# Layer norm between two attentions with tokens on partitions; softmax weights scaled by GpSimd before their transpositions

## The chip, the cores and the metric

The kernel runs on one core of a Trainium2 chip. The metric is device time in microseconds (us) of one execution, as the median of several runs.

## The reference

One layer of a first block (gated convolution, dilated attention, feed-forward) is followed by two layers of a second block, over 512 tokens of width 1024 in fp32. Three attentions over 16 heads of 64 follow each other. The first two are softmax attentions, the third is a stick-breaking one. What the change touches:

```python
# softmax attention (layers 1 and 2): per head and query, over the keys
p = exp(scores - max); o = (p @ v) / sum(p)
# layer 2: select keys, attend, gate, project, then the layer norm
p = softmax(logits); o = p @ v
x = layer_norm(ALPHA * x + (o * silu(g)) @ w_out, ln_g, ln_b)
# layer 3: stick-breaking attention on that x, its own gate, projection and layer norm

def layer_norm(x, g, b):
    mu = mean(x, axis=-1); var = mean((x - mu) ** 2, axis=-1)
    return (x - mu) * rsqrt(var + LN_EPS) * g + b
```

## The kernel before, in words

**Layout.** Activations lie with channels on partitions: eight tiles of 128 channels x 512 tokens. Every tensor that goes into a projection is kept as a pair h, l of rounded parts, and every weight block (8 x 128 rows of 128 columns) as a pair hi, lo. A chunk of a projection (`Product.chunk`, lines 302 to 304) is three matmuls, hi*h, hi*l and lo*h, and a projection of one channel tile has eight chunks.

**Weights.** The queue SP loads a block into one of two buffers `wraw`; ScalarE (ACT) rounds it to `whi` (line 120) and GpSimd (POOL) subtracts for `wlo` (line 124), in the second half of the kernel in four pieces of 256 columns. Splits run two blocks ahead of use; there are four buffers of each part.

**Order.** TensorE's (PE) order is that of the program, written out by hand. `pe` is a stream of chunks; `pe.pull(n)` issues the next n, and `pe.after(n, fn)` calls fn once n more chunks have been issued. The other engines' queues are ordered by a planner from program order and expected readiness, and each engine then works strictly in its queue's order.

**Softmax loops** (`pair_loop`, from about 184 to 390 us and 1028 to 1217 us). Eight pairs of heads, each head one slot. In a slot, the scores of its four query tiles alternate with the transpositions (`turn`) and the value products (`weigh`) of the head before, with projection chunks of coming heads pulled in between. `SoftmaxPair.weights` takes the scores to `P` with their maximum on VectorE (DVE, line 627), then ACT the exponential with its sum `den` (line 629, shown as line 193). `turn` transposes the weights of a group of key tiles on PE (line 594), group (0,) first, and ACT and DVE split the result (596, 597). `weigh` multiplies by the values (513). `joined` (519, 520) puts the two halves into `f`. The sums are handled apart: once per pair, `widen` takes the reciprocals and spreads them over 64 columns each (633, 635), `denominators` transposes them on PE (640) and copies them with a factor 0.5 (642), and `finish1` or `finish2` multiplies `f` by them (944; 1480 and 1481 with the gate).

**The layer norm between layers 2 and 3** (`Between`, from about 1217 to 1290 us). `Outward` holds the output projection in this order: four opened channel tiles, two whole ones, and the last two in two halves of 256 tokens each. Every finished tile is added to the residual (line 1212, POOL made the residual's sum in 1207), which calls `summed`. With channels on partitions a token's mean is a sum over partitions, which PE does with a matrix of ones: a provisional mean from four tiles (`middle`, 1242 and 1243), then per half the sums and squares of the shifted tiles (`shift`, 1252 to 1263; `stats`, 1286 and 1287). Each half of each tile is normalised (1299, 1300) and split (1301, 1302) for the next projection. Behind it PE computes three gate products of layer 3 in halves (`gates` with `halved`, 1140): 24 chunks per half.

**The last layer norm** (`Last`) already turns its tiles: PE transposes them (1315), ACT copies (1316), DVE takes statistics along the free axis (1322, 1344).

Of the kernel before, what the change touches and what calls it, by code (L numbers as in the profile page):

```python
# [18 lines left out]
S = 512  # L19
# [32 lines left out]
STATS = (9, 14)  # L52
# [97 lines left out]
def model_kernel(ctx: ExitStack, tc: tile.TileContext, x, norm1_g, w_in, gate_b, conv_w, conv_b, conv_norm_g,  # L150
# [21 lines left out]
    def ps_t():  # L172
        return ps("pt", 3)
# [46 lines left out]
    ones_h = const.tile([128, 128], F32R, name="ones_h")  # L220
# [203 lines left out]
    with tc.tile_pool(name="rows", bufs=1) as rows, tc.manual_schedule(engines={  # L424
# [19 lines left out]
        nc.vector.tensor_scalar(ones_h, zero128, 2.0 / D, None, op0=OP.add)  # L444
# [119 lines left out]
    class HeadPair:  # L564
# [3 lines left out]
        def __init__(self, tmps, pool, qk, v):  # L568
            self.tmps, self.pool, self.qk, self.v = tmps, pool, qk, v
            self.P, self.parts, self.o = {}, {}, {}  # L570
# [28 lines left out]
        def weigh(self, r, group):  # L599
# [17 lines left out]

    class SoftmaxPair(HeadPair):
# [11 lines left out]

        def widen(self):
            rinv = self.pool.tile([128, 2, NT], F32, name="rinv", bufs=2)
            nc.vector.reciprocal(rinv, self.den)
            self.wide = tmp(self.tmps).rearrange("p (t r d) -> p t r d", t=NT, r=2)
            nc.vector.tensor_copy(self.wide, rinv.rearrange("p r t -> p t r")[:, :, :, None].to_broadcast([128, NT, 2, 64]))

        def denominators(self):
            pb = ps_t()
            for qt in range(NT):
                nc.tensor.transpose(pb[:, 128 * qt:128 * qt + 128], self.wide[:, qt].rearrange("p a b -> p (a b)"), ident)  # L640
            self.rb = tmp(self.tmps)
            nc.scalar.activation(self.rb, pb, AF.Copy, scale=0.5)

        def ended(self):
            self.finish(self.f, self.rb)
# [21 lines left out]
    def pair_loop(pair, stream_of, pulls, last=lambda: None):  # L667


        def slot(head, turns, weighs, widen, pulls):  # L670
# [17 lines left out]
            if widen:  # L688
                widen()

        turns = weighs = [None] * 3
        for c in range(ND):
            stream_of(c)
            pr = pair(c)
            for r in range(2):
                slot((pr, r), turns, weighs, pr.widen if r else None, pulls[2 * c + r - 2 * ND] if c >= ND - 2 else pulls[0] if c or r else FIRST)
# [6 lines left out]
        slot(None, turns, weighs, None, DRAIN[1:])  # L703
# [83 lines left out]
    with tc.tile_pool(name="mix1", bufs=1) as mix1:  # L787
# [119 lines left out]
        with tc.tile_pool(name="loop1", bufs=1) as lp:  # L907
# [34 lines left out]
            def finish1(c):  # L942
                def finish(f, rb):
                    nc.vector.tensor_mul(o32[:, c, :], f, rb)
                return finish

            def pair1(c):
# [12 lines left out]
                return SoftmaxPair(lp, lp, (qk[0], qk[1]), lambda: qk["v"], lambda r, qt: B[r][:, 384 - 128 * qt:], finish1(c))  # L960
# [193 lines left out]
    def gated(pool, into, f, c, already, scale=1.0):  # L1154

        def parts():
            if not already:
                nc.vector.tensor_mul(f, f, gs[c])
# [5 lines left out]
        if already or c in gs:  # L1164
# [56 lines left out]
    class Between(Outward):  # L1221

        def summed(self, c, ts):
            part = self.part
            if c == 1:
                nc.vector.tensor_add(part, self.es[0], self.es[1])
            elif c in (2, 3):
                nc.vector.tensor_add(part, part, self.es[c])  # L1230
            if c == 3:
                h, l = act_pair(self.pool, "st", 2)
                nc.scalar.copy(h, part)
                nc.vector.tensor_sub(l, part, f32(h))
                pe.after(4, lambda: self.middle(h, l))
            self.ready.append((c, ts))
            if self.centred:
                self.shift(c, ts)

        def middle(self, h, l):  # L1240
            pm = ps_t()
            nc.tensor.matmul(pm, ones_h, h, start=True, stop=False)
            nc.tensor.matmul(pm, ones_h, l, start=False, stop=True)
            nc.scalar.copy(self.mid, pm)
            self.centred = True
            for a in self.ready:
                self.shift(*a)

        def shift(self, c, ts):
            t = slice(*ts)  # L1250
            es, s1, s2 = [e[:, t] for e in self.es], self.s1[:, t], self.s2[:, t]
            nc.vector.tensor_sub(es[c], es[c], self.mid[:, t])
            eng = nc.gpsimd if c < 4 else nc.vector
            if c == 0:
                nc.scalar.activation(s2, es[c], AF.Square)
            else:
                sq = self.pool.tile([128, S], F32, name="sq", bufs=3)[:, t]
                nc.scalar.activation(sq, es[c], AF.Square)
                if c == 5:
                    eng.tensor_add(s1, es[4], es[5])  # L1260
                elif c > 5:
                    eng.tensor_add(s1, s1, es[c])
                eng.tensor_add(s2, s2, sq)
            if c == ND - 1:
                half = TS.index(ts)
                pe.after(STATS[half], lambda: self.stats(half))

        def normed(self, pool, ys, prods):

            self.pool, self.ready, self.centred, self.ys = pool, [], False, ys  # L1270
            self.mid, self.part, self.s1, self.s2, self.var = (pool.tile([128, S], F32, name=n)
                                                               for n in ("mid", "part", "s1", "s2", "var"))
            self.run()
            for half in range(2):
                pe.together(*[p[half] for p in prods])
            pe.finish()

        def stats(self, half):
            t = slice(*TS[half])
            n = S // 2  # L1280
            p1, p2 = ps_t()[:, :n], ps_t()[:, :n]
            for p, s in ((p1, self.s1), (p2, self.s2)):
                h, l = (a[:, :n] for a in act_pair(self.pool, "st", 2))
                nc.scalar.copy(h, s[:, t])
                nc.vector.tensor_sub(l, s[:, t], f32(h))
                nc.tensor.matmul(p, ones_d, h, start=True, stop=False)
                nc.tensor.matmul(p, ones_d, l, start=False, stop=True)
            mu, var = self.part[:, t], self.var[:, t]
            nc.scalar.activation(var, p1, AF.Square)
            nc.vector.tensor_copy(mu, p1)  # L1290
            nc.vector.tensor_sub(var, p2, var)
            act(var, var, AF.Ln, bias=eps5)
            act(var, var, AF.Exp, scale=-0.5)
            for c, e in enumerate(self.es):
# [294 lines left out]
```

## Time and profile before

| | before |
|---|---|
| median of 3 runs | 1583.32 us (1580.19 to 1585.54) |
| the profiled execution | 1582.75 us |
| its span, first to last instruction | 1580.9 us |
| TensorE busy | 96% of the span |
| mean granted TensorE clock | 0.986 |

Busy time is the time in which an engine has an instruction; matmuls overlap in the pipeline, so their single durations add up to more than the time that they take. In a row, `[1.28 <-ACT Ah]` is idle time of that engine before the instruction and what ended it; `x4` stands for four instructions merged in one row.

### The profile page before, as it was taken

What the parts mean: (1) busy time and instruction counts of PE and PEld (TensorE: products, weight loads), DVE (VectorE), ACT (ScalarE), POOL (GpSimd) and SP (SyncE); (2) the same over time, 40 slices, a digit from 0 to 9 for tenths busy, and PEclk for the clock granted to TensorE, in tenths of its full rate; (3) what the DMA queues carried; (4) which work ended last, traced back from release to release, by engine and by line L of the source; (5) the groups of instructions that cost most, each with busy time, mean ns of one, the idle gap of its engine ahead of it and who ended that gap; (6) DMA issues with size and microseconds to landing.
All of it is one profiled execution on the core that took longest, in us unless ns stands there. A gap on an engine that the chain in (4) does not pass through costs nothing.

```text
span 1580.9 us, 21344 instructions
## 1 busy us (share of the span) xinstructions
PE 1519.2 (96%) x7870; PEld 1290.7 (82%) x7870; DVE 1133.5 (72%) x1867; ACT 827.1 (52%) x1495; POOL 767.0 (49%) x650
## 2 busy tenths in 40 slices
PE   7999999998999999999999989999999789999996
PEld 5888888887878888888888878888887678888885
DVE  8996578777867567627726679988887765777764
ACT  4454678777343443424424344376665445666642
POOL 3687533333735644454454464544552875334324
PEclk9999999999999999999999999999999799999998
DMA  4333321211324333243332342322220313212212
GB/s 142 91 107 93 107 68 41 80 54 54 98 75 119 108 93 89 85 120 94 93 107 87 95 121 68 93 57 78 62 59 14 95 53 94 68 54 81 67 54 80
DMA packets 234604, 130.37 MB, mean 82 GB/s; under 512 B 5206, under 2 KB 232774, under 8 KB 234500
## 3 DMA queue, kind: packets, MB, share of 16 engines
q1 hardware_dynamic: 234356, 128.75, 27.9%
q8 instruction: 62, 1.02, 0.3%
q14 instruction: 42, 0.34, 0.1%
q10 hardware_dynamic: 144, 0.26, 0.0%
HBM read 126.90 MB, written 2.10 MB: 82 GB/s over the span
## 4 chain that ended last, share of the span: by engine, by line
PE 57%; DVE 25%; ACT 8%; issue 4%; POOL 3%; DMA 3%; SPq 0%; DVEq 0%; ACTq 0%; POOLq 0%
PE pj L302 9%; PE pj L303 9%; PE pj L304 9%; DVE pt L832 6%; PE s L303 5%; PE s L302 5%; PE s L304 5%; PE o L513 3%; POOL wlo L124 2%; PE pt L594 2%; PE pj L326 2%; PE pj L328 2%; PE pj L327 2%; PE s L583 1%; DVE score L1445 1%
## 5 line engine op out<-in xcount | busy, mean ns | idle before, releaser
L124 POOL TENSOR_TENSOR wlo<-wraw,whi 128x256 fp32r<-128x256 f32 (+2 forms) x548 | 654.2, 1218 | 698.7 <-ACT whi L120 655.0
L120 ACT CAST whi<-wraw 128x1024 fp32r<-128x1024 f32 (+3 forms) x255 | 243.9, 965 | 243.9 <-PE pj L303 79.0
L302 PE MATMUL pj<-Ah,whi 128*128 128x512 f32 (+3 forms) x896 | 359.5, 401 | 3.7 <-DVE v L719 2.1
L304 PE MATMUL pj<-Ah,wlo 128*128 128x512 f32 (+3 forms) x896 | 348.3, 389 | 2.8 <-POOL wlo L124 2.8
L303 PE MATMUL pj<-Al,whi 128*128 128x512 f32 (+3 forms) x896 | 348.5, 389 | 0.0
L304 PEld LDWEIGHTS pj<-Ah,wlo 128*128 128x128 f32 (+1 forms) x896 | 168.9, 189 | 39.2 <-POOL wlo L124 4.1
L302 PEld LDWEIGHTS pj<-Ah,whi 128*128 128x128 f32 (+1 forms) x896 | 169.5, 189 | 29.1 <-DVE Al L475 1.8
L303 PEld LDWEIGHTS pj<-Al,whi 128*128 128x128 f32 (+1 forms) x896 | 169.6, 189 | 23.9
L832 DVE SCALAR_TENSOR_TENSOR pt<-S,cw,pt 128x494 f32<-128x494 f32 (+26 forms) x210 | 141.8, 733 | 5.5 <-ACT pt L825 3.5
L302 PE MATMUL s<-Ah,whi 128*128 128x512 f32 (+1 forms) x352 | 136.6, 388 | 7.8 <-ACT Ah L1301 4.0
L303 PE MATMUL s<-Al,whi 128*128 128x512 f32 (+1 forms) x352 | 136.3, 387 | 3.7 <-DVE Al L1302 3.7
L304 PE MATMUL s<-Ah,wlo 128*128 128x512 f32 (+1 forms) x352 | 135.9, 386 | 0.0
L326 PE MATMUL pj<-whi,Ah 128*128 128x256 f32 x384 | 112.4, 293 | 1.3 <-DVE q L534 1.3
L597 DVE TENSOR_TENSOR PTl<-pt,PTh 128x512 fp32r<-128x512 f32 x144 | 85.9, 597 | 32.7 <-ACT PTh L596 31.7
L328 PE MATMUL pj<-whi,Al 128*128 128x256 f32 x384 | 108.5, 282 | 0.0
L327 PE MATMUL pj<-wlo,Ah 128*128 128x256 f32 x384 | 108.3, 282 | 0.0
L193 ACT ACTIVATE P<-P,nm 128x128 f32<-128x128 f32 (+3 forms) x128 | 72.0, 563 | 62.9 <-DVE nm L627 61.7
L745 DVE SCALAR_TENSOR_TENSOR u<-ur,fw,u 128x511 f32<-128x511 f32 x44 | 74.9, 1705 | 37.5 <-ACT u L744 37.5
L302 PEld LDWEIGHTS s<-Ah,whi 128*128 128x128 f32 x352 | 68.0, 193 | 21.9 <-ACT Ah L1301 4.6
L596 ACT CAST PTh<-pt 128x512 fp32r<-128x512 f32 x144 | 73.1, 513 | 19.1 <-PE pt L594 18.7
L303 PEld LDWEIGHTS s<-Al,whi 128*128 128x128 f32 x352 | 68.1, 194 | 17.1 <-DVE Al L1302 4.6
L594 PE MATMUL pt<-ident,P 128*128 128x128 f32 x480 | 76.7, 273 | 2.5 <-ACT P L193 0.9
(334 smaller groups left out, 3181.2 us busy)
## 6 DMA issues: line engine op xcount, KB each, us to landing
wraw<-in_w_in_dram SPq DMA_DIRECT2D x56, 512.0 KB
wraw<-in_w_up_dram SPq DMA_DIRECT2D x44, 512.0 KB
wraw<-in_w_in_a_dram SPq DMA_DIRECT2D x36, 512.0 KB
wraw<-in_w_in_b_dram SPq DMA_DIRECT2D x32, 512.0 KB
wraw<-in_w_down_dram SPq DMA_DIRECT2D x16, 512.0 KB
wraw<-in_w_attn_out_dram SPq DMA_DIRECT2D x8, 512.0 KB
wraw<-in_w_conv_out_dram SPq DMA_DIRECT2D x8, 512.0 KB
wraw<-in_w_out_dram SPq DMA_DIRECT2D x8, 512.0 KB
```

Source lines behind the costliest of these rows:

```text
L120: nc.scalar.copy(h, s)
L124: nc.gpsimd.tensor_sub(l[:, k], s[:, k], h[:, k].bitcast(F32))
L302: nc.tensor.matmul(o, hv[:, k, :], ah, start=first, stop=False)
L303: nc.tensor.matmul(o, hv[:, k, :], al, start=False, stop=False)
L304: nc.tensor.matmul(o, lv[:, k, :], ah, start=False, stop=last)
L326: nc.tensor.matmul(o, ah, hv, start=k == 0, stop=False)
L327: nc.tensor.matmul(o, ah, lv, start=False, stop=False)
L328: nc.tensor.matmul(o, al, hv, start=False, stop=k == 7)
L594: nc.tensor.transpose(pt[:, at:at + 128], self.P[r][:, k0:k0 + 128], ident)
L597: nc.vector.tensor_sub(l[:, :at], pt[:, :at], f32(h)[:, :at])
L745: nc.vector.scalar_tensor_tensor(u[:, 1:], v[:, :S - 1], fw[:, 1, j:j + 1], u[:, 1:], op0=OP.mult, op1=OP.add)
L832: nc.vector.scalar_tensor_tensor(o, a, w, o, op0=OP.mult, op1=OP.add)
```

## The change

Two parts. First, in both softmax loops the weights `P` are divided by their sums before they are transposed: a reciprocal of 128x1 on VectorE and a product with two scalars on GpSimd, per head and query tile; `widen`, `denominators` and the products with the reciprocals go. Second, `Between` now works as `Last` does: a common class `Turned` transposes the tiles, takes the statistics along the free axis, and `Between.finish` normalises them with tokens on partitions; `back` transposes each channel tile back and applies gain and bias. `back(c)` is called 7 + 2c chunks after `finish`.

```diff
-STATS = (9, 14)
+BACK = (7, 2)
...
     class HeadPair:
...
         def weigh(self, r, group):
...
-                if r == 0:
+                if r == 0 and self.f is None:
                     self.f = tmp(self.tmps)
...
-        def widen(self):
-            pass
-
-        def denominators(self):
-            pass
...
     class SoftmaxPair(HeadPair):
...
             act(pp, pp, AF.Exp, bias=m, scale=-1.0, accum_out=d)
-
-        def widen(self):
...
-        def denominators(self):
...
+            nc.vector.reciprocal(d, d)
+            nc.gpsimd.tensor_scalar(pp, pp, d, 0.5, op0=OP.mult, op1=OP.mult)

         def ended(self):
-            self.finish(self.f, self.rb)
+            self.finish(self.f)
...
     def pair_loop(pair, stream_of, pulls, last=lambda: None):
...
-            if widen:
-                widen()
...
-                if r:
-                    weighs[1] = lambda pr=pr: (pr.weigh(1, GROUPS[1]), pr.denominators())
...
-            def finish1(c):
-                def finish(f, rb):
-                    nc.vector.tensor_mul(o32[:, c, :], f, rb)
-                return finish
...
+                pr.f = o32[:, c, :]
...
-    def gated(pool, into, f, c, already, scale=1.0):
+    def gated(pool, into, f, c, scale=1.0):

         def parts():
-            if not already:
-                nc.vector.tensor_mul(f, f, gs[c])
+            nc.vector.tensor_mul(f, f, gs[c])
...
-    class Between(Outward):
...
-    class Last(Outward):
+    class Turned(Outward):
...
+        def scales(self, ts):
+            rstd = self.rstd[:, ts[0]:ts[-1] + 1]
+            for t in ts:
+                nc.vector.bn_aggr(self.mv[:, t], self.stats[:, t])
+            act(rstd, self.mv[:, ts[0]:ts[-1] + 1, 1], AF.Ln, bias=eps5)
+            act(rstd, rstd, AF.Exp, scale=-0.5)
+
+    class Between(Turned):
...
+        def finish(self, ts):
+            self.scales(ts)
+            mv, rstd, off = self.mv, self.rstd, self.off
+            for t in ts:
+                nc.vector.scalar_tensor_tensor(off[:, t:t + 1], mv[:, t, 0:1], -1.0, rstd[:, t:t + 1], op0=OP.mult, op1=OP.mult)
+            for k in range(0, D, 512):
+                for t in ts:
+                    z = self.y[:, t, k:k + 512]
+                    if t % 2:
+                        nc.scalar.activation(z, z, AF.Identity, bias=off[:, t:t + 1], scale=rstd[:, t:t + 1])
+                    else:
+                        nc.vector.tensor_scalar(z, z, mv[:, t, 0:1], rstd[:, t:t + 1], op0=OP.subtract, op1=OP.mult)
+            for c in range(ND):
+                pe.after(BACK[0] + BACK[1] * c, lambda c=c: self.back(c, ts))
+
+        def back(self, c, ts):
+            if ts[0] == 0:
+                self.ys.append(act_pair(keep, "A", ND))
+            pt = ps_t()[:, :S // 2]
+            for i, t in enumerate(ts):
+                nc.tensor.transpose(pt[:, 128 * i:128 * i + 128], self.y[:, t, 128 * c:128 * c + 128], ident)
+            h, l = (a[:, 128 * ts[0]:128 * ts[-1] + 128] for a in self.ys[c])
+            g, b = lng[:, c:c + 1], lnb[:, c:c + 1]
+            e = self.pool.tile([128, S // 2], F32, name="e", bufs=3)
+            nc.scalar.activation(h, pt, AF.Identity, bias=b, scale=g)
+            if c % 2:
+                nc.scalar.activation(e, pt, AF.Identity, bias=b, scale=g)
+            else:
+                nc.vector.tensor_scalar(e, pt, g, b, op0=OP.mult, op1=OP.add)
+            nc.vector.tensor_sub(l, e, f32(h))
...
-            def finish2(c):
...
             def pair2(c):
...
-                                   lambda r, qt: maskb[:, OFF[qt]:OFF[qt] + 128 * (qt + 1)], finish2(c), 0.125)
+                                   lambda r, qt: maskb[:, OFF[qt]:OFF[qt] + 128 * (qt + 1)],
+                                   lambda f: gated(dp, og, f, c), 0.125)
```

## Rows read from the trace of the kernel before

**Rows 1.** The page's first part: busy us, share of the span, instructions.

```profile
PE 1519.2 (96%) x7870; PEld 1290.7 (82%) x7870; DVE 1133.5 (72%) x1867; ACT 827.1 (52%) x1495; POOL 767.0 (49%) x650
```

**Rows 2.** Windows: loop 1's body, loop 2's tail, the layer norm; columns as headed.

```profile
core 0: us, PE busy (x) PEld busy (x) DVE busy (x) ACT busy (x) POOL busy (x), PEclk, DMA share, GB/s
184.00:340.00 156.00, 154.95 (x935) 136.02 (x934) 118.98 (x247) 123.20 (x263) 60.09 (x74) 1.00 0.22 65
...
1185.00:1217.00 32.00, 30.20 (x166) 24.38 (x165) 23.20 (x54) 20.44 (x50) 4.31 (x4) 1.00 0.06 17
...
1217.00:1290.00 73.00, 58.27 (x328) 51.73 (x327) 57.08 (x82) 29.28 (x50) 55.50 (x57) 0.86 0.20 58
```

**Rows 3.** Waits of PE, 1217 to 1290 us: total us, times, longest.

```profile
PE pt L1286 <- ACT sth L1284: 5.1, 2, 4.7
PE s L302 <- ACT Ah L1301: 4.0, 3, 2.2
PE s L303 <- DVE Al L1302: 3.7, 4, 1.6
...
```

**Rows 4.** Chain of waits (start, us) at line 640; the group of the copy of line 642.

```profile
1213.20 0.46 PE pt L640 x4
...
L642 ACT ACTIVATE tmp<-pt 128x512 f32<-128x512 f32 x16 | 9.3, 584 | 4.3 <-PE pt L640 4.3
```

**Rows 5.** Timeline of an ordinary slot of loop 2: start us, us, instruction.

```profile
1108.85 0.19 ACT L193 ACTIVATION_READ_ACCUMULATOR P<-P,nm 128x1 f32 x1
...
1111.67 0.60 PE L594 MATMUL pt<-ident,P 128*128 128x128 f32 x4
```

**Rows 6.** Groups of POOL operations by form: busy us, mean ns.

```profile
L1207 POOL TENSOR_TENSOR S<-Ah,Al 128x512 f32<-128x512 f32 x8 | 10.4, 1294 | 57.1 <-DVE tmp L1480 57.1
...
L438 POOL TENSOR_SCALAR ident<-jp 128x128 f32<-128x128 int32 x1 | 0.6, 567 | 0.0
L795 POOL IOTA dist_i<- 128x512 int32 x1 | 0.6, 555 | 0.0
```

**Rows 7.** Timeline of a slot of loop 1 with a weight run ahead on POOL.

```profile
202.99 3.45 POOL L124 TENSOR_TENSOR wlo<-wraw,whi 128x256 fp32r<-128x256 f32 x4 [5.62 <-ACT whi L120]
203.68 0.18 ACT L193 ACTIVATION_READ_ACCUMULATOR P<-P,nm 128x1 f32 x1
206.68 0.60 PE L594 MATMUL pt<-ident,P 128*128 128x128 f32 x4
```

**Rows 8.** Timeline of a slot in loop 2's tail.

```profile
1193.19 0.65 PE L594 MATMUL pt<-ident,P 128*128 128x128 f32 x4
...
1193.26 0.19 ACT L193 ACTIVATION_READ_ACCUMULATOR P<-P,nm 128x1 f32 x1
```

**Rows 9.** Timeline: one DVE product twice, and a POOL sum.

```profile
1186.94 1.30 POOL L1207 TENSOR_TENSOR S<-Ah,Al 128x512 f32<-128x512 f32 x1 [1.51 <-DVE tmp L1480]
...
1187.84 0.95 DVE L1481 TENSOR_TENSOR tmp<-tmp 128x512 f32<-128x512 f32 x1
...
1201.38 0.68 DVE L1481 TENSOR_TENSOR tmp<-tmp 128x512 f32<-128x512 f32 x1
```

**Rows 10.** Chain of waits, one matmul of each width; a window of low clock.

```profile
1205.33 0.23 PE pj L304
...
1286.02 0.12 PE s L304
...
1258.00:1266.00 8.00, 6.32 (x31) 6.02 (x32) 8.00 (x14) 2.88 (x7) 5.32 (x7) 0.57 0.29 88
```

**Rows 11.** Timeline of the last layer norm's statistics.

```profile
1562.88 0.38 PE L1315 MATMUL pt<-ident,e 128*128 128x128 f32 x2
...
1564.83 0.21 ACT L193 ACTIVATE rstd<-rstd 128x2 f32<-128x2 f32 x1
```

**Rows 12.** Groups on DVE, 1217 to 1290 us: busy us, mean ns.

```profile
L1300 DVE SCALAR_TENSOR_TENSOR S<-S,vec,var 128x256 f32<-128x256 f32 x16 | 13.9, 915 | 0.0
L1302 DVE SCALAR_TENSOR_TENSOR Al<-S,vec,Ah 128x256 fp32r<-128x256 f32 x16 | 10.4, 691 | 0.2 <-ACT Ah L1301 0.2
```

More of the change, by code (lines that the diff above doesn't have):

```diff
@@ L443, in model_kernel @@
         nc.vector.tensor_scalar(ones_d, zero128, 1.0 / D, None, op0=OP.add)
-        nc.vector.tensor_scalar(ones_h, zero128, 2.0 / D, None, op0=OP.add)
         nc.vector.tensor_scalar(ones_b, zero128, 0.0, None, op0=OP.add)
@@ L629, in weights @@
             act(pp, pp, AF.Exp, bias=m, scale=-1.0, accum_out=d)
-        def widen(self):
[L632 to L635, printed above, removed]
-        def denominators(self):
[L638 to L642, printed above, removed]
+            nc.vector.reciprocal(d, d)
+            nc.gpsimd.tensor_scalar(pp, pp, d, 0.5, op0=OP.mult, op1=OP.mult)
         def ended(self):
-            self.finish(self.f, self.rb)
+            self.finish(self.f)
     class StickPair(HeadPair):
@@ L667, in pair_loop, with slot @@
     def pair_loop(pair, stream_of, pulls, last=lambda: None):
-        def slot(head, turns, weighs, widen, pulls):
+        def slot(head, turns, weighs, pulls):
             def step(fn):
@@ L1162, in parts @@
             into.append((h, l))
-        if already or c in gs:
+        if c in gs:
             parts()
@@ L1219, in run @@
                 pe.skewed(p)
-    class Between(Outward):
[L1225 to L1294, printed above, removed]
-                e, g, b = e[:, t], lng[:, c:c + 1], lnb[:, c:c + 1]
-                if half == 0:
-                    self.ys.append(act_pair(keep, "A", ND))
-                h, l = (a[:, t] for a in self.ys[c])
-                (nc.gpsimd if c > 2 else nc.vector).tensor_sub(e, e, mu)
-                nc.vector.scalar_tensor_tensor(e, e, g, var, op0=OP.mult, op1=OP.mult)
-                nc.scalar.activation(h, e, AF.Identity, bias=b)
-                nc.vector.scalar_tensor_tensor(l, e, b, f32(h), op0=OP.add, op1=OP.subtract)
@@ L1326, in summed, with buffers @@
             pe.after(4, turn)
-        def normed(self, pool):
+        def buffers(self, pool):
             self.pool = pool
@@ L1333, in normed @@
             self.rstd = pool.tile([128, NT], F32, name="rstd")
+        def scales(self, ts):
[5 more added lines that the diff above has]
+    class Between(Turned):
+        def normed(self, pool, ys, prods):
+            self.buffers(pool)
+            self.off = pool.tile([128, NT], F32, name="off")
+            self.ys = ys
+            self.run()
+            for half in range(2):
+                pe.together(*[p[half] for p in prods])
+            pe.finish()
+        def finish(self, ts):
[27 more added lines that the diff above has]
+            nc.vector.tensor_sub(l, e, f32(h))
@@ L1334, in normed @@
+    class Last(Turned):
+        def normed(self, pool):
+            self.buffers(pool)
             self.g, self.b = (pool.tile([128, D], F32, name=n) for n in "gb")
@@ L1340, in finish @@
         def finish(self, ts):
-            mv, g, b = self.mv, self.g, self.b
-            rstd = self.rstd[:, ts[0]:ts[-1] + 1]
-            for t in ts:
-                nc.vector.bn_aggr(mv[:, t], self.stats[:, t])
-            act(rstd, mv[:, ts[0]:ts[-1] + 1, 1], AF.Ln, bias=eps5)
-            act(rstd, rstd, AF.Exp, scale=-0.5)
-            rstd = self.rstd
+            self.scales(ts)
+            mv, rstd, g, b = self.mv, self.rstd, self.g, self.b
             for t in ts:
```

18 lines of the change are left out of this document (6 added, 12 removed).

## The prediction

> **What bounds the kernel now.** The page comes first: TensorE (PE) is busy for 96% of the span, VectorE (DVE) for 72%, GpSimd (POOL) for 49% [rows 1]. An average over stages says little about one stage, so next come windows cut at the stages that the change touches [rows 2]. In the body of the first softmax loop PE is busy for 154.95 of 156 us: there an instruction less on PE is time gained. In the tail of the second loop, where no projection is left to fill in, it is busy for 30.20 of 32 us. In the layer norm between the last two attentions it is busy for 58.27 of 73 us, so it waits for 14.7, at a granted clock of 0.86, while DVE is busy for 57.08. The waits of PE in that stage say on whom [rows 3]: 5.1 + 4.0 + 3.7 us in the three longest kinds, all behind ScalarE (ACT) or DVE. So two things are asked: what new wait the loops get, and what the layer norm loses.
>
> **Loops: what goes.** Each of the 16 pairs of heads loses four PE transpositions of the widened reciprocals (line 640). Four such take 0.46 us on PE between their neighbours (1213.20 to 1213.66) [rows 4], so 16 x 0.46 = 7.4 us go. This PE time is on the path, because PE is full. With them go per pair an ACT copy (0.58) [rows 4] and, on DVE, a reciprocal, a broadcast and one product. DVE (119 us busy in the 156 of rows 2) and ACT lie beside PE, so I count these at nothing; in the tails, where their chain sets the pace, they may give back 1 to 2 us.
>
> **Loops: what comes.** Each head gets, for each of four query tiles, a DVE reciprocal of 128x1 and a POOL product over 128, 256, 384 or 512 columns, between the exponential and the transposition. The first transposition group of the next slot reads key tile 0 of all four query tiles, so only the last and widest (512) can be late. I followed it in all 32 slots. One ordinary slot: the exponential's sum is read out at 1108.85 + 0.19 = 1109.04, first transposition at 1111.67 [rows 5]. Transpositions follow each other every 0.11 us, so the fourth, the one that needs the last tile, comes at 1112.0, and at 1111.5 once the four of line 640 ahead of it are gone. There are 2.5 us for a reciprocal (0.2 with its hops) and the product.
>
> What does the product cost? No row of before shows it for 512 columns of fp32. From above, the two-input operation of this width takes 1.294 us; from below, an iota that only writes 512 columns takes 0.555; the one tensor_scalar in the trace, on integers, takes 0.567 for 128 columns, which times four is 2.27 [rows 6]. I take 0.93, midway between no input and two inputs, because the product reads one; 2.27 stays as the upper end.
>
> The Trainium skill (GPSIMD Engine Reference, section 4.1, Engine selection) says that on GpSimd a one-input elementwise operation runs at about line rate, while a two-input one takes about twice VectorE's time. No run here shows the first; by it the product would lie near the iota's row, and the sum below would be about -13 us (estimated).
>
> At 0.93 us the 32 slots fall into three kinds. (a) 16 slots have room as above and cost nothing. (b) In 9 slots a run of four weight pieces stands ahead on POOL, which works in order: in one the sum is out at 203.68 + 0.18 = 203.86 and the reciprocal done by 204.3 behind a running DVE operation, but the weight run that began at 202.99 ends at 206.44, so the product ends near 207.4, against a fourth transposition at 206.68 + 0.33 = 207.0 [rows 7]. The nine cost 0.3 to 0.8, together 4.7 us. (c) Seven slots, the four last of loop 1, two of the last three of loop 2 and the first of loop 2 (which has a weight run ahead), have next to no room: the last sum of one of them is read out at 1193.26 + 0.19 = 1193.45, and PE is already in the group that began at 1193.19 [rows 8]. There reciprocal and product come on top almost whole: 0.6 to 1.7, together 8.9 us. The sum is 13.6 us; the same count gives 8 us with a product of 0.555, 20 with 1.294 and 41 with 2.27. A stalled PE lets DVE catch up, which would shrink it; I leave that out. The loops: 13.6 - 7.4 = +6 us.
>
> The weight splits of line 124 stand behind the products now: the four products of a slot cover 1280 columns, 1280 / 512 x 0.93 = 2.3 us in some 12.4 us, or 29 us in the 156 of rows 2, where POOL is busy for 60. It stays under 60% busy there, and the splits run two blocks ahead, so I count that at nothing; if the cover is gone, PE waits at line 304 for one piece, a quarter of a 3.45 us run [rows 7]. In loop 2 POOL also holds eight sums of line 1207, which wait for a gate's buffer; its release moves from line 1480 to line 1158, behind the join of the pair, about 2 us later. A product queued behind one of them is late by that.
>
> **Layer norm.** The stage is the window of 73 us in rows 2; it ends with the six halved gate products. PE's work in it, by code: 60 matmuls of 512 columns at 0.23 and 240 of 256 columns at 0.12 [rows 10], with 10 for the sums of about 2 us: 44.6 us, and some 2 us of neighbours at its ends. Beside the 14.7 us of waits, that leaves 11 to 12 of the 58.27 busy us to a low clock: the grant is 0.57 from 1258 to 1266, right behind the longest waits [rows 10], and 0.86 over the stage.
>
> The change takes the ten sum matmuls out (2 us) and puts 64 transpositions in, at 0.11 each 7.1 us: 49.7 us of PE work, 52 with the neighbours. The statistics move to bn_stats on DVE, as the last layer norm does already: from its two last transpositions at 1562.88 over copy, two bn_stats, two aggregates, logarithm and exponential to 1565.04 is 2.2 us [rows 11], and a normalising pass over 512 columns, about the 0.58 of rows 4 with its hop, makes 3.0. PE has seven chunks of 3 x 0.12 between, 2.6 us: a wait of half a microsecond at the first half, in place of most of the 12.8 us of rows 3. DVE, which sets the end of each half, loses the 16 + 16 operations of lines 1300 and 1302 (24.3 us) [rows 12] and the shifts and sums of lines 1252 to 1263 and 1299; it gets per half about two normalising passes of 512, four affine copies and eight differences of 256 columns at 0.4, some 6 us, spread over 16 chunks of PE work. For the second half all this lies beside the first half's gate products (24 chunks, 9 us), so its waits should go whole.
>
> What is late next is the third gate weight: its slot comes free when the halved product of channel 6 is done, and its copy and a split run like that of rows 7 then take over 4 us; I allow 1 to 2 us of wait. With another 1 to 2 for hops and 2 to 4 of low clock the stage takes 57 to 62 us, a gain of 11 to 16; I take 14. The bounds: 8, if more than half of the waits and of the low clock stay; 19, if none do.
>
> **Sum.** +6 - 14 = -8 us on the profiled execution (1582.75 us, of which 1580.9 are span), less a little for the terms left out: -7. The profiled time is 0.6 us under the median of the runs shown, 1583.32; on that I forecast 1576.
>
> **Rivals.** One, on the other side: the POOL product is slow. At 2.27 us the loops cost 41 - 7.4 = +33, less 14: +19, about 1602. For it speaks the only tensor_scalar row; against it, that this row converts integers and compares. It decides from about 1.6 us on, where the 32 slots cost 26 us and the sum reaches +5. Chance 0.20, with lesser prices from 1588 up.
>
> Two: the gains cancel. A product of 1.3 us gives 20 - 7.4 - 14 = -1; the same comes if the layer norm gains only 8. Or POOL and DVE disturb each other: the same DVE product took 0.68 us at 1201.38 and 0.95 at 1187.84, when a POOL sum was running (1186.94 to 1188.24) [rows 9]. If, by estimate, a third of DVE's time in the loops goes to operations on two SBUF operands (the splits of q and k, the rotary products) and a fifth of that falls beside the 32 x 2.3 = 75 us of new POOL work and is stretched by 40%, that is some 8 us of DVE time over both loops, of which 3 may reach PE, and slower products add 2: sum -2. Chance of this group 0.25.
>
> The Trainium skill (SBUF — State Buffer, section Who interferes with whom) states that a VectorE instruction with two SBUF inputs contends with a GpSimd instruction that reads SBUF; the pair of rows agrees (0.68 against 0.95 us).
>
> Three: the product runs near the iota's 0.555 us and the layer norm gains 17: 8 - 7.4 - 17 = -16, 1567. Chance 0.10. The forecast itself (1569 to 1579) has 0.45.
>
> **Numbers.** A measurement here can tell 0.3%, about 4.7 us, from no change. Faster by more: 0.45 + 0.10 = 0.55; within: 0.25; slower: 0.20. The range that should hold the time 8 times in 10 reaches from 1564 (all of the third rival) to 1594 (half of the first); the forecast's own is 1569 to 1579.
>
> **What would show it.** In the profile after: POOL's product of 512 columns near 0.9 us; PE waits before line 594, on POOL, of some 14 us, more than half of them in the tails; body windows of the loops shorter or equal; no wait of PE over 1 us in the layer norm but one at the first half's turn back, and a granted clock above 0.95 there; the stage 11 to 16 us shorter. I am wrong if PE's waits on POOL exceed 25 us, if the products stand behind line 1207, or if PE still waits in the layer norm for ACT or DVE as it did.

## The result, and the profile after

The changed kernel takes 1564.38 us (median of 4 runs, 1563.22 to 1564.60), the kernel before beside it 1583.10 us (4 runs). The ratio is 0.9881 with a 95% interval of [0.9864, 0.9899]: 18.7 us faster, where 7 were forecast. The profiled execution's span went from 1580.9 to 1562.8 us.

The page's first part after, to lay beside [rows 1]:

```profile
PE 1505.7 (96%) x7860; PEld 1281.4 (82%) x7860; DVE 1104.2 (71%) x1923; ACT 821.9 (53%) x1483; POOL 827.2 (53%) x765
```

PE is 13.5 us less busy with ten instructions fewer, and span less PE busy, its idle time, fell from 61.7 to 57.1 us. POOL has 115 instructions more, 60 us of work, and nobody's share changed much. (PEld is TensorE's loading of weights.)

Windows after, of the stages of [rows 2]: loop 1's body, loop 2's tail and the layer norm, whose window is now 56 us long:

```profile
184.00:340.00 156.00, 153.04 (x917) 134.15 (x916) 120.42 (x282) 122.34 (x261) 92.21 (x123) 1.00 0.22 65
1182.00:1214.00 32.00, 29.25 (x158) 23.79 (x157) 21.18 (x59) 19.61 (x47) 11.95 (x17) 1.00 0.06 17
1214.00:1270.00 56.00, 51.87 (x372) 47.87 (x371) 31.86 (x59) 28.89 (x52) 35.95 (x45) 1.00 0.27 76
```

In the two loop windows PE waits more than before (3.0 us against 1.0, 2.8 against 1.8) while POOL gained 32 us in the first. VectorE's load in the body is about where it was (120.4 against 119.0): keep that number, the explanation comes back to it. In the layer norm 4.1 us of waits stand where 14.7 were, and the granted clock is 1.00 instead of 0.86.

Waits of PE in the layer norm after (total us, times, longest), for [rows 3]:

```profile
PE pt L1265 <- ACT y L1254: 1.9, 1, 1.9
PE pt L1265 <- DVE y L1256: 1.1, 1, 1.1
PE pt L1205 <- DVE S L1185: 0.8, 1, 0.8
PE pt L1265 <- DVE e L1273: 0.2, 1, 0.2
```

Waits of PE over the whole span after, the kinds that the loops have. `PTh` and `PTl` are the two parts into which the turned weights are split. Line numbers are those of each run's own kernel: the transpositions of line 594 are line 592 here.

```profile
PE pt L592 <- POOL P L623: 7.7, 13, 2.0
...
PE o L511 <- ACT PTh L594: 4.2, 2, 3.5
...
PE o L511 <- DVE PTl L595: 3.5, 7, 1.7
```

The first line is the new wait, for the product; its forecast was 13.6. The product itself, by form, where [rows 6] had only neighbours (busy us, mean ns):

```profile
L623 POOL TENSOR_SCALAR P<-P,den 128x512 f32<-128x512 f32 x32 | 28.1, 879 | 30.1 <-DVE den L622 23.5 <-PE pj L302 4.4 <-PE pt L592 2.2
L623 POOL TENSOR_SCALAR P<-P,den 128x384 f32<-128x384 f32 x32 | 20.3, 633 | 27.8 <-DVE den L622 27.7
L623 POOL TENSOR_SCALAR P<-P,den 128x256 f32<-128x256 f32 x32 | 18.3, 572 | 36.6 <-DVE den L622 36.6
L623 POOL TENSOR_SCALAR P<-P,den 128x128 f32<-128x128 f32 x32 | 16.8, 526 | 23.0 <-DVE den L622 20.7 <-PE pj L303 1.6 <-PE s L581 0.7
```

Where the 18.1 us of span went, by marks in the two traces: from loop 2's last score product to loop 3's first it was 113.4 us (1202.46 to 1315.84) and is 97.8 (1199.87 to 1297.64), 15.6 less. At loop 2's last score product the changed kernel is 2.6 us ahead, and that is what the two loops and the stages between them gave.

### The profile page after: what moved, and what is told of

It is laid out like the page before. It is cut to its first block, busy times and chain, and to the rows that moved or that the text cites. A ratio compares the mean times of both kernels' runs of the same rounds, so it can differ in the third digit from the quotient of the medians.

```text
span 1562.8 us, 21533 instructions
## 1 busy us (share of the span) xinstructions
PE 1505.7 (96%) x7860; PEld 1281.4 (82%) x7860; DVE 1104.2 (71%) x1923; ACT 821.9 (53%) x1483; POOL 827.2 (53%) x765
## 4 chain that ended last, share of the span: by engine, by line
PE 61%; DVE 21%; ACT 6%; POOL 4%; issue 4%; DMA 2%; SPq 0%; DVEq 0%; ACTq 0%; POOLq 0%
PE pj L301 10%; PE pj L302 10%; PE pj L303 10%; DVE pt L809 6%; PE s L301 6%; PE s L302 6%; PE s L303 6%; POOL wlo L124 3%; PE pt L592 2%; PE o L511 2%; PE pj L325 2%; PE pj L327 2%; PE pj L326 2%; ACT whi L120 2%; PE s L581 1%
## 5 line engine op out<-in xcount | busy, mean ns | idle before, releaser
L124 POOL TENSOR_TENSOR wlo<-wraw,whi 128x256 fp32r<-128x256 f32 (+2 forms) x548 | 644.9, 1202 | 548.4 <-ACT whi L120 513.8
L623 POOL TENSOR_SCALAR P<-P,den 128x128 f32<-128x128 f32 (+3 forms) x128 | 83.2, 652 | 117.6 <-DVE den L622 108.5
L592 PEld LDWEIGHTS pt<-ident,P 128*128 128x128 f32 x480 | 60.7, 141 | 26.9 <-POOL P L623 11.1
```

The lines of the kernel that those rows point to most:

```text
L124: nc.gpsimd.tensor_sub(l[:, k], s[:, k], h[:, k].bitcast(F32))
L592: nc.tensor.transpose(pt[:, at:at + 128], self.P[r][:, k0:k0 + 128], ident)
L623: nc.gpsimd.tensor_scalar(pp, pp, d, 0.5, op0=OP.mult, op1=OP.mult)
```

## Experiments

Each was timed in five rounds against the kernel before on its own chip; the diffs are against the changed kernel unless said otherwise. A run and the changed kernel were not timed in one series, and the kernel before itself had medians from 1581.70 to 1584.17 us in these series: differences of less than about 2.5 us between two runs are not told by their medians.

**The two halves alone.** `e1` is the layer norm with the old softmax (line 623's product and line 622's reciprocal out, `widen` and `denominators` back); `e2` is the kernel before with only the softmax's part of the change.

> The layer norm with tokens on partitions alone; the softmax loops and their sums as in the kernel before. Theory A (the two parts add, the layer norm's 15.4 us in the trace are its own): 1583 - 15.4 = 1567.5 us, two thirds to nine tenths of the whole gain. Theory B (the forecast's step: the layer norm gains 14 and the loops are what I mis-sized): 1569, hardly apart from A here, so scale_only decides between them. Rival C (the parts help each other, for instance through the weights that arrive earlier): 1573 or more. In the trace the stage from the last score product of loop 2 to the first of loop 3 should take about 98 us against 113 before.

> The scaled softmax weights alone; the layer norm as before. The forecast's count (13.6 us of new waits against 7.4 us of transpositions saved): about 1589 us, slower by 6. The trace of the changed kernel (7.7 us of waits on GpSimd, 7.4 us of PE work saved, slots shorter by 0.4 to 0.9 us where VectorE was late before): 1580 to 1582, faster by 1 to 3. Rival: all of the whole gain beyond the layer norm's 14 comes from here: 1578.

Measured: e1 1567.70 us, ratio 0.9913 [0.9899, 0.9926], 14.5 us less than before (1582.22). e2 1580.26, ratio 0.9987 [0.9978, 0.9996], 2.0 less. The two add to 16.5 of the 18.7. So the layer norm's 14 were right, and the +6 of the loops was the wrong term. In the two loops (182 to 412 and 1020 to 1217 us) PE waits 10.1 us in the trace before and 16.3 in that of e2: 6.2 more, where 13.6 were forecast. Over the whole span it is busy for 8.1 us less (1519.2 and 1511.1). The waits of PE in e2:

```profile
PE pt L594 <- POOL P L625: 7.5, 13, 1.8
PE pt L1299 <- ACT sth L1297: 7.4, 2, 6.3
```

The new wait has the size that it has in the changed kernel (7.5 us in 13 places), so it doesn't depend on the layer norm; the second line is the old layer norm's wait of [rows 3].

**The transpositions alone.**

```
+    pb = ps_t()          # once per pair, where denominators() was
+    for qt in range(NT):
+        nc.tensor.transpose(pb[:, 128 * qt:128 * qt + 128], ident, ident)
```

> The changed kernel, with the four transpositions per pair put back as idle work (of a constant, nobody reads them), and nothing else of the old sums. Theory (PE is full in the loops, so its 64 x 0.115 us count whole, less where a wait on GpSimd stands right behind and swallows them): +6 to +7.4 us over the changed kernel's 1564.4, so 1570.5 to 1571.8. Rival (the saving came from ACT and VectorE work that went with them, and PE had room): +0 to +3, 1564 to 1567.

Measured: 1570.63 us, ratio 0.9923 [0.9910, 0.9937], 6.2 us over the changed kernel, against the 7.4 counted. That term stands.

**The product twice.**

```
             nc.gpsimd.tensor_scalar(pp, pp, d, 0.5, op0=OP.mult, op1=OP.mult)
+            nc.gpsimd.tensor_scalar(pp, pp, one1, 1.0, op0=OP.mult, op1=OP.mult)
```

> The changed kernel with a second GpSimd product of the same shape (by ones) behind each of the 128. Theory (PE waits for the last product of a head: each of the 13 late slots gets later by the whole second product of 0.9 to 1.1 us, and four more slots with 0.3 to 0.6 us of room become late by 0.4): +13 to +16 us, about 1579. The forecast's count of slots at 1.76 us instead of 0.88 gives the same, +16. Rival (the planner orders GpSimd's queue anew and hides most of it): +3 to +6, 1569. A second rival (GpSimd full, weight splits late, PE waits at line 303 as well): +25 or more.

Measured: 1587.67 us, ratio 1.0043 [1.0031, 1.0056], 23 us over the changed kernel, more than the theory's 16 and less than the second rival's 25. Its waits on the product, and the second product's group:

```profile
PE pt L594 <- POOL P L626: 26.7, 19, 3.5
```

```profile
L626 POOL TENSOR_SCALAR P<-P,one 128x512 f32<-128x512 f32 x32 | 24.3, 759 | 3.0
```

A second 0.76 us raised the waits by 19.0 us to 26.7. The prediction's first rival has 26 us of waits and +5 for the whole change at a product of about 1.6 us; the two products together take 0.88 + 0.76 = 1.64, and this run has 26.7 and stands 5.4 over the kernel before. The count's level is met there, its slope is not: from 0.88 to 1.64 us it rises by some 14 us, and 19.0 were measured. The first rival's mechanism is real: it only needed a price that the product does not have.

The time rose by 4 us more than the waits. In this profile PE's idle time is 16.3 us longer than in the changed kernel's (73.4 against 57.1), and the mean granted clock is 0.986 against 0.994, by which some 13 us more are lost (an estimate). In six places of the two loops the granted clock falls to the lower of its two levels, 1.2 GHz, at or shortly behind the end of a wait for the product: the window from 260 to 270 us, with a wait of 2.17 that ends at 263.1, has a clock of 0.83. Two waits of 1.98 and 1.97 us have no such loss behind them.

**The product of 512 columns on VectorE.**

```
-            nc.gpsimd.tensor_scalar(pp, pp, d, 0.5, ...)
+            (nc.vector if qt == NT - 1 else nc.gpsimd).tensor_scalar(pp, pp, d, 0.5, ...)
```

> The changed kernel, but the 32 products of 512 columns (one per score slot, the one for which TensorE was seen to wait) go to VectorE; the other 96 stay on GpSimd. Theory (TensorE waits for GpSimd's product 7.7 us in 13 waits, because the product stands behind a low-part subtraction of 2.45 us or takes 0.88 us where only 0.5 us is there): those waits go nearly whole, VectorE takes some 0.5 to 0.7 us per slot that it has, so 1557 to 1561 us, and the waits on POOL P fall under 2 us. Rival 1: VectorE runs in order and is 70% busy; 32 products of 0.5 to 0.75 us push its low parts (PTl) back, and new waits on PTl of 6 us or more take the place: 1563 to 1572. Rival 2 (the waits are not on the path, other waits take them up): 1564, no change, with waits of the same sum elsewhere.

Measured: 1565.17 us, ratio 0.9891 [0.9876, 0.9906]: no gain. The time lies in the first rival's range, the waits are as the second rival said. Waits of PE from 184 to 412 us, loop 1:

```profile
PE o L511 <- ACT PTh L594: 4.6, 3, 3.1
PE o L511 <- DVE PTl L595: 2.7, 4, 1.7
PE pt L592 <- DVE PTl L595: 0.9, 3, 0.4
PE pt L592 <- DVE P L623: 0.8, 2, 0.5
PE pj L301 <- DVE v L696: 0.6, 3, 0.2
```

The 3.6 us that loop 1 waited for POOL's product became 0.8 for VectorE's, and 2.2 us of waits for low parts and values that VectorE now makes later took most of their place. The sum of the waits in this stretch is 9.6 us, in the changed kernel 9.7; the 6 us of new waits on `PTl` that the first rival wanted are not there.

**Later norm of the last keys, later turns back.**

```
-   pe.after(12 if c < 1 else 8, lambda: norm(raw, h, l))
+   pe.after(12 if c < 1 else 9 if c == ND - 1 else 8, lambda: norm(raw, h, l))     # e6
-BACK = (7, 2)
+BACK = (10, 1)                                                                     # e7
```

> The changed kernel, with the key's normalization of the last pair of the first attention left until 9 chunks after its product instead of 8; by the order of the instructions ScalarE then has the first half's cast PTh of 256 columns ahead of the table load (1.28 us) and the four casts of k (2.53 us), as it had in the kernel before. Theory: the one wait of TensorE of 3.46 us on PTh in the tail of the first loop, which only the change brought in, goes; 1561 to 1562.5 us. Rival: what is late then is the cast of k or the values behind it, and the wait only moves: 1564 to 1565.

> The changed kernel, with the turns back of the new layer norm begun 10 chunks (and one more for each) after the statistics instead of 7 (and two more for each). Theory: the two waits of TensorE for the normalized rows (1.9 us on ScalarE's, 1.1 us on VectorE's) are filled with chunks of the products beside them; 1561.5 to 1563.5 us. Rival: the products that follow need the turned-back halves, and come to wait for them by as much: 1564 to 1566.

Measured: e6 1562.78 us, ratio 0.9875 [0.9860, 0.9890]; e7 1565.70, ratio 0.9895 [0.9878, 0.9912]. e6 lies between its theory's range and its rival's. The wait of 3.5 us on PTh is gone and one for the cast of k stands in its place (340 to 365 us), in part as its rival had it:

```profile
PE s L578 <- ACT k L557: 2.0, 1, 2.0
PE o L511 <- DVE PTl L595: 1.3, 1, 1.3
PE pt L592 <- POOL P L623: 0.9, 1, 0.9
```

From its first score product (line 578) to its last, loop 1 takes 192.3 us before, 193.2 in the changed kernel and 190.4 in e6. Of the last step 1.7 us is the low clock that the changed kernel has from 360 to 370 us (0.84) and e6 has not (1.00).

In e7 the rival held. The layer norm's waits moved (1214 to 1270 us): 1.3 us to the low halves that the gate products read, and 1.4 to VectorE's operation on a turned-back half (line 1273):

```profile
PE pt L1265 <- DVE e L1273: 1.4, 1, 1.4
PE s L302 <- DVE Al L1274: 1.3, 1, 1.3
PE pt L1205 <- DVE S L1185: 0.8, 1, 0.8
PE pt L1265 <- ACT y L1254: 0.7, 1, 0.7
...
```

**The old VectorE and ScalarE work put back.** This is the run that found the failed step.

```
+   def widen(self):                 # after the pair's last slot
+       nc.vector.tensor_copy(wide, den.to_broadcast(...))
+   def denominators(self):          # no transpositions
+       nc.scalar.activation(rb, wide, AF.Copy, scale=0.5)
    def ended(self):
+       nc.vector.tensor_mul(wide, self.f, rb)
```

> The changed kernel, with the VectorE and ScalarE parts of the old division put back without its transpositions: for each pair of heads in the two softmax loops one VectorE copy of 512 columns (0.61 us in the kernel before), one VectorE product of 512 columns (0.69 us) and one ScalarE copy of 512 columns from SBUF, all in their old places; what they compute is not used. Theory A (the loops' gain beside the transpositions is not from the relief: TensorE's new waits were simply fewer than forecast, 7.7 us instead of 13.6, and old waits of 0.9 us went): 1564 to 1566 us, at most 1.5 us over the changed kernel. Theory B (the relief of VectorE and ScalarE gave the loops 3 to 4 us): 1567 to 1569 us, with new waits of TensorE on PTl and PTh of 3 us or more.

Measured: 1572.63 us, ratio 0.9940 [0.9927, 0.9954], 8.2 us over the changed kernel. Theory A falls. Theory B was right in its direction, too small in its size, and wrong about the place: PE does not wait for PTl and PTh, but for the product. The page's first part and the waits of PE:

```profile
PE 1513.0 (96%) x7860; PEld 1286.4 (82%) x7860; DVE 1126.1 (72%) x1955; ACT 830.1 (53%) x1499; POOL 834.8 (53%) x765
```

```profile
PE pt L592 <- POOL P L623: 13.6, 15, 2.1
...
PE o L511 <- DVE PTl L595: 3.0, 4, 1.6
```

13.6 us, the forecast's own figure: the nine slots behind a weight run add to 5.2 (4.7 forecast), and five of the seven without room to 8.4 (8.9 forecast for all seven; one of the five has two waits). That the sums agree to a tenth is luck; by kind they agree within half a microsecond. The product itself is also longer here, 0.925 us on the average against 0.879: in four slots of the loops' tails it runs beside the VectorE copy that was put back and takes 0.93 instead of 0.69.

Where the time goes, from the first score product of a loop to its last: loop 1 takes 193.2 us in the changed kernel and 193.8 here, loop 2 176.3 and 182.0. In loop 1 the new waits are set off by the wait on PTh of 3.5 us, of which 0.5 is left.

The idle time of PE is hardly larger than in the changed kernel (1570.8 - 1513.0 = 57.8 against 57.1); instead PE is busy 7.3 us longer with as many instructions. That is clock. Three windows of 10 us of this run, and three at the same places of the work in the changed kernel:

```profile
376.00:386.00 10.00, 8.23 (x37) 6.44 (x36) 6.76 (x13) 6.74 (x12) 3.37 (x3) 0.83 0.18 53
458.00:468.00 10.00, 7.53 (x20) 5.68 (x21) 5.09 (x8) 2.20 (x3) 2.72 (x2) 0.66 0.35 106
1202.00:1212.00 10.00, 7.89 (x36) 6.75 (x36) 8.01 (x22) 7.18 (x17) 5.14 (x7) 0.83 0.01 2
```

```profile
376.00:386.00 10.00, 8.23 (x43) 6.42 (x43) 7.15 (x13) 9.10 (x17) 5.13 (x4) 1.00 0.33 90
455.00:465.00 10.00, 7.28 (x24) 5.61 (x25) 5.30 (x8) 2.19 (x3) 2.92 (x2) 0.83 0.35 105
1196.00:1206.00 10.00, 8.51 (x48) 6.87 (x48) 6.67 (x21) 7.60 (x18) 4.64 (x7) 1.00 0.01 2
```

The first and third lose 0.17 x 10 = 1.7 us each that the changed kernel does not lose, and the second 1.7 more. In the third lies this run's longest wait for the product, 2.1 us before 1204.5, and in the first one of 1.0 before 379.2. The second lies behind loop 1 and behind a wait of 3.6 us that the changed kernel has too (3.1); e5, e7 and e12, which are no slower than 1566 us, lose as much there, so it need not be the edit's. A fourth such loss lies at 20 to 30 us, ahead of all that was edited, and e7, e9 and e10 have it as well. So of the clock 3.4 us stand beside the product's waits (e10 has the first of the two as well), and this one profile does not take the 8 us apart. The granted clocks of all executions are 0.990 to 0.992 here and 0.992 to 0.994 in the changed kernel: by them 3 to 4 us of the 8 are clock on the average (an estimate), and the rest is time at full clock.

**Which engine's relief.** `e9` is e8 without the ScalarE copy; `e10` goes the other way and deletes line 622.

```
-            nc.vector.reciprocal(d, d)
```

> The run that put the old VectorE and ScalarE work back cost 8 us over the changed kernel. This is the same without its ScalarE copy: per pair only the two VectorE instructions (0.67 and 0.69 us) are put back. Theory (the product on GpSimd stands at the end of a chain TensorE, VectorE, ScalarE, VectorE, GpSimd, and each us that VectorE has less to do in a slot brings the product forward, so that TensorE waits less for it): nearly all of the 8 us stay, 1570 to 1573 us, with waits on POOL P of 11 to 14 us against 7.7. Rival (the relief is ScalarE's, whose copy stands ahead of the exponential and the PTh casts): 1564 to 1567 us, waits on POOL P under 9 us.

> The changed kernel without its 128 reciprocals: the weights are multiplied by their sums instead of divided by them. That takes 128 x 0.163 us = 21 us off VectorE, and VectorE out of the chain between ScalarE's exponential and GpSimd's product. Theory (VectorE's relief comes back to TensorE through the product): waits on POOL P fall from 7.7 us to 3 to 5 us, 1558 to 1562 us. Rival (those 7.7 us that are left are GpSimd's own, its product behind a run of weight parts; VectorE no longer decides): waits on POOL P within 1 us of 7.7, 1563.5 to 1565 us.

Measured: e9 1574.13 us, ratio 0.9935 [0.9921, 0.9948], with this first line of waits:

```profile
PE pt L592 <- POOL P L623: 12.2, 15, 2.0
```

So the relief is VectorE's; ScalarE's copy, 0.63 us in e8, was free. In e9 loop 1 takes 194.0 us and loop 2 180.1, and from loop 2's last score product to loop 3's first it is another 3.2 more than in the changed kernel. PE's idle time is 60.9 us, 3.8 longer. So in both runs most of the price is paid from loop 2 on. e10, whose output is no softmax any more: 1563.88 us, ratio 0.9873 [0.9859, 0.9886], with

```profile
PE pt L592 <- POOL P L622: 5.9, 10, 1.9
```

VectorE is busy for 1087.8 us, 16 less than in the changed kernel, and that gives 0.5 us by the medians, within the rival's bounds; the waits fell by 1.8, between what theory and rival said. By the marks loop 1 is 1.5 us shorter than in the changed kernel (191.7) and loop 2 1.2 (175.1), while the profile's mean clock is 0.991 against 0.994. So the relief is worth between nothing and some 3 us, and the two directions are not alike: 22 us more (e8, e9) cost 8 to 10, 16 less give little. These three loads differ in more than their amount. e8 and e9 put back two instructions of 0.67 and 0.69 us per pair, e10 takes out eight of 0.16; whether the amount decides, or the length and the place of the pieces, was not tried.

**The product on VectorE only where PE waits.** Both are e6 with a product of 512 columns moved to VectorE only where PE waits for it: e11 in seven slots, e12 in one.

```
-   nc.gpsimd.tensor_scalar(pp, pp, d, 0.5, ...)
+   (nc.vector if (r, qt) == (self.vec, NT - 1) else nc.gpsimd).tensor_scalar(pp, pp, d, 0.5, ...)
+   # e11: vec=1 for pairs 0 to 5 of loop 1, vec=0 for pair 0 of loop 2; e12: the latter alone
```

> The changed kernel with the later norm of the last keys (9 chunks), and with the product of 512 columns on VectorE only for the seven heads whose product stands behind a run of weight parts on GpSimd: the second head of the first six pairs in the first loop, and the first head of the first pair in the second. Theory: of the 1.97 + 0.85 + 0.5 + 0.5 + 3 x 0.3 us that TensorE waits there most goes, on top of the later norm's 1.6 us: 1559 to 1561.5 us, faster than both kernels. Rival (as with all 32 on VectorE, its low parts come later by as much): 1562 to 1564 us.

> The changed kernel with the later norm of the last keys (9 chunks), and one single product of 512 columns on VectorE, that of the first head of the second loop's first pair, for which TensorE waits 1.97 us; the six of the first loop stay on GpSimd. By the profiles the later norm alone moved the end of the loops 2.7 us forward against the changed kernel, and the one product 0.7 us. Theory (the two gains lie in different places and add): 1560 to 1562 us, the wait of 1.97 us down to 0.5. Rival (something behind the slot is then late, or the gains of the profile are no more than the scatter of 1.5 us between runs): 1562 to 1564 us.

Measured: e11 1562.53 us, ratio 0.9864 [0.9851, 0.9878]; e12 1562.18 us, ratio 0.9869 [0.9853, 0.9886]. Both lie in their rivals' ranges. In e12 the wait of 1.97 us fell to 0.44, and its profile lost e6's gain again in the tail of loop 1, at a clock of 0.68 where e6 has 1.00:

```profile
360.00:370.00 10.00, 9.27 (x38) 7.86 (x38) 4.40 (x13) 5.41 (x13) 3.85 (x4) 0.68 0.00 0
```

The medians of e6, e11 and e12 lie 1.6 to 2.2 us under the changed kernel's; their intervals overlap its own. They beat the kernel before by far more than the intervals; that they beat the changed one is not shown.

## Why the prediction was wrong

**Where it failed: the loops, at the words on VectorE and ScalarE, "so I count these at nothing; in the tails, where their chain sets the pace, they may give back 1 to 2 us".** Per pair VectorE loses a copy of 0.59 us, a product of 0.69 and a reciprocal of 0.20, 1.5 us, and gets eight reciprocals of 0.16, 1.3 us. Three groups of the trace before (the product of loop 1; loop 2's, line 1480, has 692 ns as well) and one of the trace after:

```profile
L635 DVE COPY tmp<-rinv 128x512 f32<-128x512 f32 x16 | 9.5, 593 | 0.2
L944 DVE TENSOR_TENSOR o<-tmp 128x512 f32<-128x512 f32 x8 | 5.5, 692 | 0.4
L633 DVE RECIPROCAL rinv<-den 128x8 f32<-128x8 f32 x16 | 3.2, 200 | 9.1 <-ACT P L193 9.1
```

```profile
L622 DVE RECIPROCAL den<-den 128x1 f32<-128x1 f32 x128 | 20.4, 159 | 30.4 <-ACT P L193 29.4
```

The load stays about where it was (119.0 and 120.4 us of 156). The prediction took the waits from the slack of the trace before, with the old work still in it, and laid the reciprocals on top: one side of an even trade was charged and the other was not. e8 is the kernel of that count: waits on the product 13.6 us as forecast, and with the layer norm's 14.5 taken out of its 1572.6 the loops cost 1572.6 - 1567.7 = +4.9, forecast +6. The removal took that back: 7.7 us of waits, and loops at -2.0 (e2). The omission that the prediction did name, "A stalled PE lets DVE catch up", is in e8 too, and the sum of its waits is not smaller for it.

**Why the tail of the sum is more than the waits.** A wait can cost more than its length: in the third window of e8 the clock takes 1.7 us beside the wait's 2.1, and in e4 it falls at or behind six waits for the product, and not behind two others as long as some of them. The prediction priced the low clock in the layer norm and nowhere else.

**What held.** The transpositions: 7.4 counted, 6.2 measured (e3). The product of 512 columns: 0.93 taken, 0.879 measured; the kind (b) slots 4.7 against 3.7 and (c) 8.9 against 4.0, summed from the single waits; the runs of four pieces that make kind (b) stand in loop 1 too, not only in the second half of the kernel. "More than half of them in the tails" did not hold: 2.0 of the 7.7 us lie in the last slots of the loops (6.5 of 13.6 in e8). The splits' cover held: POOL is busy for 92.2 us of the 156, 59%, where "under 60%" was said. No product came late behind a gate's base sum: the two waits for it over 0.8 us (1.97 and 0.84) stand behind weight runs.

**Layer norm.** -14 forecast, -14.5 alone, -15.6 in the trace. In the trace 14.7 - 4.1 = 10.6 us of waits went, and 0.14 x 73 = 10.2 to the low clock; the 5.1 us of added PE work (7.1 less 2, as counted) come off, which makes 15.7. "No wait of PE over 1 us in the layer norm but one at the first half's turn back" was nearly right: 1.9 us there, and one of 1.1 at the second half, which the prediction had put at none. The wait for the third gate weight, allowed 1 to 2 us, is not there. The clock above 0.95 is there (1.00).

**The rivals.** The slow product would have needed nearly twice the price (e4). The third rival, 8 - 7.4 - 17, came nearest in time, for another reason: its waits of 8 us were reached with a product of 0.88, not 0.555. Of the second rival the contention is visible. VectorE's two-input group of the norm's low parts, 184 to 340 us, before and after:

```profile
L933 DVE TENSOR_TENSOR stl<-tmp,sth 128x512 fp32r<-128x512 f32 x13 | 12.9, 993 | 0.6
```

```profile
L910 DVE TENSOR_TENSOR stl<-tmp,sth 128x512 fp32r<-128x512 f32 x13 | 14.2, 1093 | 0.7
```

The 1.3 us more lie in three of the 13 instructions, 0.67 us before with next to nothing on POOL beside them and 1.11 after, beside POOL's product. One of them, in the trace before and in that after, with the product:

```profile
231.78 0.67 DVE L933 TENSOR_TENSOR stl<-tmp,sth 128x512 fp32r<-128x512 f32 x1
```

```profile
231.22 1.11 DVE L910 TENSOR_TENSOR stl<-tmp,sth 128x512 fp32r<-128x512 f32 x1
231.76 1.12 POOL L623 TENSOR_SCALAR P<-P,den 128x512 f32<-128x512 f32 x1
```

The other ten took 1.04 to 1.12 us before as after, beside the weight parts that POOL makes in both kernels. The price of it is in the loops' measured sum already. The Trainium skill (SBUF — State Buffer, section Who interferes with whom) has a VectorE instruction with two SBUF inputs contend with GpSimd's reads; these rows agree (0.67 against 1.11 us).

**What stays open.** That PE's path turns on the VectorE work that went was seen in e8 and e9; by which instruction in which slot was not taken apart, nor whether its amount or its place decides. Each profile is one execution, in which losses of 1.7 us to the clock come and go. The halves alone give 16.5 of the 18.7 us; the 2.2 between lie within the intervals of the three ratios.

## What to carry to other kernels

When an edit removes and adds work on the same in-order engine, recompute the slack with both before you price the new waits. An engine that is busy for three quarters of a stage does not have the last quarter to give: here 22 us put back cost 8 to 10, though 16 taken out gave little. Look behind a new wait for what the clock loses there, as well as at its length. And moving the late instruction to the neighbour engine moved the waits with it (e5); moving only one took that wait from 1.97 to 0.44 us (e12), but its gain is too small for the medians.

## What was not expected of the hardware

The product of 512 columns has two durations. In all ten cases where it starts straight behind a weight run on POOL it takes 1.12 to 1.14 us; in 18 of the 22 others 0.69 or 0.70, and in the last four 1.06 to 1.19. The timeline of POOL after, the slot of [rows 7] and one without a run:

```profile
203.17 3.46 POOL L124 TENSOR_TENSOR wlo<-wraw,whi 128x256 fp32r<-128x256 f32 x4 [0.41 <-ACT whi L120]
206.62 1.12 POOL L623 TENSOR_SCALAR P<-P,den 128x512 f32<-128x512 f32 x1
...
359.38 0.69 POOL L623 TENSOR_SCALAR P<-P,den 128x512 f32<-128x512 f32 x1 [0.96 <-DVE den L622]
```

So the price was highest in slots that had little room. It is not the run ahead that makes the 0.43 us, as far as the trace tells: the four others have no run ahead of them. What all fourteen long ones have, and none of the eighteen short ones, is a VectorE instruction with two SBUF operands at the same time, as in the pair of rows at 231 us above. One without a run, with VectorE's instruction beside it:

```profile
243.98 0.67 DVE L924 SCALAR_TENSOR_TENSOR B<-dist,lnc 128x512 f32<-128x512 f32 x1
244.16 1.06 POOL L623 TENSOR_SCALAR P<-P,den 128x512 f32<-128x512 f32 x1 [2.21 <-PE pj L302]
```

In all fourteen the product begins while such an instruction runs and ends 0.56 us after it (here 245.22 against 244.65), as if most of it stood still until then. In three of them a second such instruction begins beside the product: it takes 1.07 us and ends 0.54 after the product. So the contention that the second rival looked for on VectorE's side lengthens the product too; no run was made to move the two apart.

The Trainium skill (GPSIMD Engine Reference, section 4.1, Engine selection) puts a one-input operation near line rate; by it the prediction estimated the product near the iota's 0.555 [rows 6]. Without such an instruction beside it it took 0.69 or 0.70, with one 1.06 to 1.19, both above that estimate.
